# A fused attention, RWKV and feed-forward block on one core: packing small products by quadrant, storing q and k once, and reordering gate and exponential work

## The chip, the cores and the metric

The kernel runs on one core of a Trainium2 chip. The metric is device time in microseconds (us) of one execution. TensorE (PE) does the matrix products, its weight loads (PEld) run beside them; VectorE (DVE) and ScalarE (ACT) read PSUM and do the elementwise work; GpSimd (POOL) and SyncE (SP) issue the DMAs, and POOL does some elementwise work on SBUF.

## The reference

One block of depth 1 on a sequence of 1024 tokens and a width of 1024, in fp32:

```
mod = silu(c) @ w_mod + b_mod                  # six vectors: shift, scale, gate, twice
u   = rms_norm(x) * (1 + scale1) + shift1
proj = u @ w_in                                # q, k, v, f | r, k, v, w, a, g | two gates
o_fox  = causal softmax(q k^T / 8 + cumsum(log f) differences) @ v          # 8 heads of 64
o_rwkv = for each token: state = state * w + (state a) b + v k;  y = state r  # 8 heads of 64
         then a group norm of y, a bonus term and a gate
merged = sigmoid(gate_fox) * (o_fox @ w1) + sigmoid(gate_rwkv) * (o_rwkv @ w2)
h = x + gate1 * (merged @ w_o)
h = h + gate2 * ((silu(conv3(a)) * b) @ w_down)  # a, b = split(modulated rms_norm(h) @ w_up)
out = rms_norm(h) * final_g
```

## The kernel before

Large products are made of two fp32r pieces per operand (`hi`, `lo`) and three 128x128x512 matmuls per tile (`gemm_steps`). The feed-forward block uses seven products per 2x2 block (`OPS`, keys 1 to 7), run by a written list `plan`; `T1` to `T4` are sums of its inputs that are made while the first products run.

The recurrence runs in eight units: four pairs of heads `p` times two halves `hf` of 512 tokens, each half eight chunks of 64 tokens (`NCU` = 8). For each unit there are two generators. `pre` makes decays (`el`, `en` are exponentials of the running sum `cum`), the scaled vectors `ar` and `bk`, the products `p1` of `bk` with `ar` (tile `p` in the trace), and a 31-step elimination on DVE (`t<-E,M` and `E<-E,t`, "the elimination" below), which goes through DRAM before it (`sm`, `M32`) and after it (`se`, `TT`). `main` then does, in this order: a transpose `X` of `TT`, the small products `xi` and `zi`, the products `uw` (copied to `Wt` by DVE and to `UV` by ACT), the products `mz` (read by DVE into `Zt` and `Mt`), the products `sp` and `yp`, and the state chain: for each chunk one product `sp<-S,Mt` on PE and one scaled copy `S` on ACT, each waiting for the one before.

`uw` and `mz` are 16 products each per unit, one for each chunk `c` and head `h`: 64 rows of contraction, 64 output rows, 128 columns, in plain fp32, and the trace shows two matmul records for each. Head 0 lies in partitions 0 to 63 and head 1 in 64 to 127 (`HS`), of the operands and of the PSUM tile alike. Two PSUM tiles are used, the first for chunks 0 to 3, the second for 4 to 7.

The order on PE is fixed by `Weave`: each generator yields how long it would wait, and the time is filled with steps of a queue of large products: first `rkv_items` (r, k, v of the next pair) and `qk_steps` (q and k of attention), then `v_steps`, then the sixteen `gate_steps`, of which the last seven run inside the attention phase (`late_gate`, tile `rk_ps`). On the other engines a scheduler orders the instructions ahead of time, and manual dependencies can pin them; within the attention and the feed-forward phases the written order holds for DVE and ACT.

`qk_steps` leaves a `hi` and a `lo` tile per half (`qh`, `ql`; two buffers with the tag `sp0`) and SP stores them to `d_st` in the layout that attention reads: three copies of 128 rows, each as two DMAs of 64 rows. `load_head` on POOL reads one head back as `stA`, `stB` and `vh`. `gate_steps` evacuates a gate's PSUM bank on ACT and DVE into a tile `gs` with the same tag `sp0`, and stores it to `d_gate`.

Of the kernel before, what the change touches and what calls it, by code (L numbers as in the profile page):

```python
# [9 lines left out]
F32 = mybir.dt.float32  # L10
# [6 lines left out]
S = 1024  # L17
# [115 lines left out]
def hybrid_block(ctx: ExitStack, tc: tile.TileContext, a, out):  # L133
# [13 lines left out]
    def f32(ap):  # L147
        return ap.bitcast(F32)
# [94 lines left out]

    marks = {}
    late_lo = deque()

# [80 lines left out]
    def gate_steps(w, i, pps, ptag, pool, tag):  # L327
        if weave.late == 1:
            yield from late_gate(w, i)
            return  # L330
        for hf in range(2):
            cs = slice(hf * NH, hf * NH + NH)
            ps = pps.tile([128, NH], F32, tag=ptag, name=f"gt{i}_{hf}")
            yield from gemm_steps(ps, w, u, cs)

            g = pool.tile([128, NH], F32, tag=tag, name=f"gs{i}_{hf}")
            nc.scalar.activation(g, ps, AF.Abs)
# [8 lines left out]
    with ExitStack() as es:  # L346
# [39 lines left out]
        def qk_steps(w, i):  # L386
            sc_ = 0.125 if i < 4 else 1.0
            for hf in range(2):
# [6 lines left out]
                stt(lo, ps, sc_, f32(hi), op0=ALU.mult, op1=ALU.subtract)  # L395
                h0 = 2 * (i % 4)
                for t, k, r0 in ((hi, 0, 0), (lo, 0, 64), (hi, 2, 0)) if i < 4 else ((hi, 1, 0), (hi, 1, 64), (lo, 3, 0)):
                    for h in range(2):
                        nc.sync.dma_start(f32(d_st[h0 + h, k, r0 : r0 + 64, cs]), f32(t[h * 64 : h * 64 + 64, :]))

# [157 lines left out]
        with tc.tile_pool(name="lg", bufs=1, reuse_waits="tile") as lg, \  # L558
# [65 lines left out]
            def forget():  # L624
# [10 lines left out]
                for hf in range(2):  # L635
# [27 lines left out]
                    nc.scalar.activation(r[:, 5, :], f32(r[:, 1, :]), AF.Copy, scale=-1.0)  # L663
                    nc.sync.dma_start(f32(d_st[:, 2, 64:68, cs]), f32(r[:, 0:4, :]))
                    nc.sync.dma_start(f32(d_st[:, 3, 64:68, cs]), f32(r[:, 2:6, :]))

# [31 lines left out]
        def pre(k, p, hf):  # L698
# [22 lines left out]
            nc.scalar.activation(en, cum, AF.Exp, scale=DEC)  # L721
            ksq = tmp("ksq")
# [58 lines left out]
            for s in range(31):  # L781
                J, W = s // 4 + 1, 31 - s
                tv = t32[:, 0 : J * W].rearrange("p (j w) -> p j w", w=W)
                tt(tv, E32[:, 0:J, s : s + 1].to_broadcast([128, J, W]),  # L784
                   M32[:, s : s + 1, s + 1 : 32].to_broadcast([128, J, W]), op=ALU.mult)
                tt(E32[:, 0:J, s + 1 : 32], E32[:, 0:J, s + 1 : 32], tv, op=ALU.add)  # L786
# [36 lines left out]
            nc.vector.tensor_copy(QA[:, :, 0, :], c3(q))  # L823
# [3 lines left out]
            tt(bon, bp, vv, op=ALU.mult)  # L827
            units[p, hf] = dict(ready=ready, pcd=pcd, ar=ar, E=E, QA=QA, TT=TT, bon=bon, UV=UV)

        def main(k, p, hf):  # L830
# [31 lines left out]
            Wt = rw.tile([128, NCU, CH], F32, tag="Wt", name=f"Wt{n}", bufs=1)  # L862
            for c0 in range(0, NCU, 4):
                ps = gen(f"uw{n}{c0}")
                for c in range(c0, c0 + 4):
                    for h in range(2):
                        x = (c - c0) * 128
                        mm(ps[HS[h], x : x + 128], TT[HS[h], c, :], QA[HS[h], c, :, :], start=True, stop=True)
                pv = ps.rearrange("p (c a s) -> p c a s", a=2, s=CH)
                nc.vector.tensor_copy(Wt[:, c0 : c0 + 4, :], pv[:, :, 1, :])  # L870
# [4 lines left out]
            for c0 in range(0, NCU, 4):  # L875
                ps = gen(f"mz{n}{c0}")
                for c in range(c0, c0 + 4):
                    for h in range(2):
                        x = (c - c0) * 128
                        mm(ps[HS[h], x : x + 128], Wt[HS[h], c, :], E[HS[h], c, h, 1:3, :], start=True, stop=True)  # L880
                pv = ps.rearrange("p (c a s) -> p c a s", a=2, s=CH)
                tt(Zt[:, c0 : c0 + 4, :], pv[:, :, 0, :], ar[:, 1, c0 : c0 + 4, :], op=ALU.add)
                for h in range(2):
                    tt(Mt[HS[h], c0 : c0 + 4, HS[h]], pv[HS[h], :, 1, :],
                       ident[HS[h], HS[h]].unsqueeze(1).to_broadcast([64, 4, CH]), op=ALU.add)
# [13 lines left out]
            for c in range(last_c + 1):  # L899
                if S[c] is not None:  # L900
                    mm(sp[:, c, :], Mt[:, c, :], S[c], start=False, stop=c == last_c, more=True)
                S.append(rw.tile([128, CH], F32, tag="state", name=f"S{n}{c}", bufs=8))
                marks["S"] = nc.scalar.activation(S[-1], sp[:, c, :], AF.Copy, scale=pcd[:, c : c + 1])
                if c + 1 < NCU:
# [82 lines left out]
    es = ExitStack()  # L987
    at = es.enter_context(tc.tile_pool(name="at", bufs=2, reuse_waits="tile"))
    pl = es.enter_context(tc.tile_pool(name="pl", bufs=2, space=PS))
    pt = es.enter_context(tc.tile_pool(name="pt", bufs=2, space=PS))  # L990
    heads = {}

    def load_head(h):
        A = at.tile([128, 2, S], F32R, tag="stA", name=f"stA{h}")
        nc.gpsimd.dma_start(A, d_st[h, 0:2, :, :].rearrange("k r s -> r k s"))
        B = at.tile([128, 2, S], F32R, tag="stB", name=f"stB{h}")
        nc.gpsimd.dma_start(B[0:68, :, :], d_st[h, 2:4, 0:68, :].rearrange("k r s -> r k s"))
# [1040 lines left out]
```

## Time and profile before

| | us |
|---|---|
| median of three runs | 1654.52 |
| the three runs | 1647.03, 1654.52, 1655.5 |
| the profiled execution | 1648.91 |
| its span | 1647.1 |
| PE busy, share of the span | 1607.8, 98% |
| DVE busy | 1222.6, 74% |
| ACT busy | 820.9, 50% |
| mean clock granted to TensorE | 0.995 |

A row of the timeline is: start in us, length in us, engine, line of the kernel, operation, tile written and tiles read, shape, count; in brackets the idle time of that engine just before it and what ended it. Rows that follow each other with the same text are merged. A group's row has its count, then the busy time and the mean length of one in ns. A row of the waits has the waiting engine and tile, who was waited for, the time in us, how often, and the longest one. From about 160 to 600 us the recurrence runs, from 628 to 820 us attention, and after 1000 us the feed-forward block.

### The profile page before, as it was taken

The page shows a single profiled execution, that of the slowest core. Times are in us where ns is not written, and L with a number is a line of the kernel's source. Part 1 is how long each engine was busy: PE and PEld are TensorE (multiplying, and loading weights), DVE is VectorE, ACT ScalarE, POOL GpSimd, SP SyncE. Part 2 cuts the span into 40 slices and gives each one's busy share as a digit, 9 for nine tenths or more (in the row PEclk, how much of TensorE's full clock was granted, in tenths as well). Part 3 has the DMA queues.
Part 4 walks back from the last instruction along what each step waited for, and adds up shares of the span by engine and source line. Part 5 has one row for each costly group of instructions (what it writes and reads, how often), then busy time and mean ns, then how long its engine had stood idle before and what let it go on. Part 6 is the DMA issues. An engine that isn't in the chain of part 4 may idle for free.

```text
span 1647.1 us, 25947 instructions
## 1 busy us (share of the span) xinstructions
PE 1607.8 (98%) x9694; PEld 1339.6 (81%) x9694; DVE 1222.6 (74%) x2373; ACT 820.9 (50%) x1537; POOL 130.8 (8%) x153
## 2 busy tenths in 40 slices
PE   7999999999999999999999999999999999999998
PEld 7777788798978788888888888788888888888886
DVE  5786787878876526888679447887777777886677
ACT  5563335445445646766623235644444444555455
POOL 0011101111111010221022000000000000000000
PEclk9999999999999999999999999999999999999999
DMA  8488645543332346433197420242232232675363
GB/s 339 138 326 242 178 123 143 134 123 94 107 115 85 97 126 157 129 117 106 56 353 270 168 81 26 84 134 97 96 119 98 96 109 96 225 254 160 122 211 109
DMA packets 121645, 240.59 MB, mean 146 GB/s; under 512 B 40048, under 2 KB 48880, under 8 KB 121520
## 3 DMA queue, kind: packets, MB, share of 16 engines
q1 hardware_dynamic: 113040, 220.58, 41.0%
q0 software_dynamic: 8480, 18.37, 4.2%
q8 instruction: 76, 1.25, 0.3%
q14 instruction: 49, 0.40, 0.1%
HBM read 173.35 MB, written 65.54 MB: 145 GB/s over the span
## 4 chain that ended last, share of the span: by engine, by line
PE 58%; DVE 5%; ACT 2%; DMA 2%; issue 1%; SPq 0%; ACTq 0%; DVEq 0%
PE X L141 13%; PE D L141 13%; PE Y L141 6%; PE wo L141 5%; PE br L141 4%; PE rk_ps L141 3%; PE W L141 3%; PE gt L141 3%; PE lg L141 2%; PE ov L141 2%; PE tp L145 2%; DMA d_gate<-gs 1%; DVE nm L1049 1%; DVE P L1059 1%; DVE tl L1089 0%
## 5 line engine op out<-in xcount | busy, mean ns | idle before, releaser
L141 PE MATMUL D<-op,op 128*128 128x512 f32 x924 | 209.8, 389 | 0.0
L141 PEld LDWEIGHTS D<-op,op 128*128 128x128 f32 x924 | 173.3, 188 | 36.3 <-DVE op L1261 0.3
L141 PE MATMUL X<-T_m,S 128*128 128x512 f32 x440 | 107.8, 390 | 1.6 <-ACT T_m L1722 1.1
L141 PEld LDWEIGHTS X<-T_m,S 128*128 128x128 f32 x440 | 82.4, 188 | 20.4 <-ACT T_m L1722 2.5
L1260 ACT CAST op<-g 128x512 fp32r<-128x512 f32 x77 | 47.8, 621 | 73.8 <-PE D L141 49.0
L1261 DVE TENSOR_TENSOR op<-g,op 128x512 fp32r<-128x512 f32 x77 | 53.0, 688 | 41.4 <-ACT op L1260 41.4
L1519 DVE SCALAR_TENSOR_TENSOR c<-ab,vec,c 128x512 f32<-128x512 f32 x88 | 65.9, 750 | 18.4 <-ACT c L1522 16.8
L784 DVE TENSOR_TENSOR t<-E,M 128x60 f32<-128x60 f32 (+24 forms) x248 | 55.6, 224 | 27.9 <-DMA M<-sm 21.8
L1485 DVE TENSOR_TENSOR A<-ur,A 128x512 fp32r<-128x512 f32 x64 | 44.0, 688 | 38.7 <-ACT A L1481 38.5
L1485 DVE TENSOR_TENSOR S<-ur,S 128x512 fp32r<-128x512 f32 x66 | 45.5, 691 | 35.2 <-ACT S L1481 35.1
L274 DVE TENSOR_TENSOR lo_in<-raw_in,hi_in 128x512 fp32r<-128x512 f32 x84 | 56.7, 712 | 17.6 <-PE gt L141 4.8
L1481 ACT CAST S<-ur 128x512 fp32r<-128x512 f32 x66 | 41.0, 622 | 55.8 <-DVE ur L1474 30.6
L141 PE MATMUL Y<-T_h,S 128*128 128x512 f32 x264 | 63.6, 390 | 0.4 <-ACT T_h L1740 0.4
L141 PE MATMUL Y<-T_h,A 128*128 128x512 f32 x264 | 63.7, 389 | 0.3 <-ACT T_h L1722 0.3
L1053 ACT ACTIVATE P<-lg,nm 128x896 f32<-128x896 f32 (+3 forms) x64 | 47.4, 743 | 30.7 <-DVE nm L1049 22.5
L1481 ACT CAST A<-ur 128x512 fp32r<-128x512 f32 x64 | 39.6, 622 | 43.1 <-PE X L141 31.3
L786 DVE TENSOR_TENSOR E<-E,t 128x60 f32<-128x60 f32 (+24 forms) x248 | 56.2, 227 | 6.4
L141 PE MATMUL W<-B_f,A 128*128 128x512 f32 x252 | 60.6, 389 | 0.0
L141 PE MATMUL X<-B_b,A 128*128 128x512 f32 x252 | 60.5, 389 | 0.0
L141 PEld LDWEIGHTS Y<-T_h,S 128*128 128x128 f32 x264 | 49.5, 188 | 11.1 <-ACT T_h L1740 0.8
L141 PEld LDWEIGHTS Y<-T_h,A 128*128 128x128 f32 x264 | 49.5, 188 | 10.9 <-ACT T_h L1722 0.7
L272 ACT CAST hi_in<-raw_in 128x1024 fp32r<-128x1024 f32 x42 | 43.8, 1048 | 26.3 <-PE ps_rkv L141 11.3
(483 smaller groups left out, 4134.4 us busy)
## 6 DMA issues: line engine op xcount, KB each, us to landing
raw_in<-in_w_in SPq DMA_DIRECT2D x50, 512.0 KB, 4.0
wm<-in_w_mod SPq DMA_DIRECT2D x48, 512.0 KB, 7.3
ur<-in_w_up SPq DMA_DIRECT2D x44, 512.0 KB, 3.8
g<-d_g SPq DMA_DIRECT2D x35, 512.0 KB, 4.0
d_g<-gs SPq DMA_DIRECT2D x44, 256.0 KB, 2.0
d_g<-c SPq DMA_DIRECT2D x33, 256.0 KB, 4.4
d_st<-qh SPq DMA_DIRECT2D x64, 128.0 KB, 2.5
stA<-d_st POOLq DMA_DIRECT2D x8, 1024.0 KB, 6.9
```

The lines of the kernel that those rows point to most:

```text
L141: nc.tensor.matmul(o, lhsT, rhs, start=start, stop=stop, skip_group_check=more)
L145: nc.tensor.transpose(o, i, eye)
L272: nc.scalar.copy(hi, raw)
L274: nc.vector.tensor_tensor(lo[:, c : c + NH], raw[:, c : c + NH], f32(hi[:, c : c + NH]), op=ALU.subtract)
L784: tt(tv, E32[:, 0:J, s : s + 1].to_broadcast([128, J, W]), M32[:, s : s + 1, s + 1 : 32].to_broadcast([128, J, W]), op=ALU.mult)
L786: tt(E32[:, 0:J, s + 1 : 32], E32[:, 0:J, s + 1 : 32], tv, op=ALU.add)
L1053: nc.scalar.activation(e[:, 0:n], lg[:, 0:n], AF.Exp, bias=nm[:, 0:1], accum_out=nm[:, 1:2])
L1260: nc.scalar.copy(hi, src)
L1261: tt(lo, src, f32(hi), op=ALU.subtract)
L1481: nc.scalar.copy(hi, src)
L1485: tt(lo, src, f32(hi), op=ALU.subtract)
L1519: stt(c, ab[:, x + hf * NH : x + hf * NH + NH], V("conv_w", 22 * x + i), c, op0=ALU.mult, op1=ALU.add)
```

## The change

1. `uw` and `mz`: odd chunks write the other half of PSUM's partitions (head 0 to partitions 64 to 127), and the two PSUM tiles now hold the even and the odd chunks. The products alternate between them. The readers follow: for odd chunks each half is read by an instruction of its own, with a shift of 64 partitions. The diff below shows `uw`; `mz` with `Zt` and `Mt` changes in the same way.
2. `d_st` becomes `d_qk`, which holds each `hi` and `lo` tile once, in one DMA of 128 rows, and `d_f` for the forget terms. `load_head` puts the layout together with four DMAs where it had two.
3. `el` and `en` of the next unit, and the last exponential of a gate, are put behind an instruction `S` of a state chain that is under way (`behind_state`, `state_done`): the gate's behind the next `S`, `el` and `en` behind the last.
4. One copy inside `bk` goes from ACT to POOL. In the first unit the first step of the elimination is put behind two DVE instructions (`after_this`).
5. The gates that run after the recurrence but before attention take their `gs` tiles from the attention pool (tag `Ps`), and start behind the gate before.
6. In `plan`, the product (1, 4) is put ahead of (0, 5).

```
     d_gate = dr.tile([16, 128, S], F32, name="d_gate")
-    d_st = dr.tile([8, 4, 128, S], F32R, name="d_st")
+    d_qk = dr.tile([4, 4, 128, S], F32R, name="d_qk")
+    d_f = dr.tile([8, 2, 4, S], F32R, name="d_f")
...
+    def after_this(i):
+        for x in first_step:
+            tc.add_manual_dep(x.ins, i.ins.name, NOSYNC)
+    held = {False: [], True: []}
+    def behind_state(i, next_one=False):
+        if marks.get("chain"):
+            held[next_one].append(i)
+        elif "S" in marks:
+            tc.add_manual_dep(i.ins, marks["S"].ins.name, NOSYNC)
+    def state_done(i, last):
+        marks["S"], marks["chain"] = i, not last
+        for x in held[True] + (held[False] if last else []):
+            tc.add_manual_dep(x.ins, i.ins.name, NOSYNC)
...
-            g = pool.tile([128, NH], F32, tag=tag, name=f"gs{i}_{hf}")
-            nc.scalar.activation(g, ps, AF.Abs)
+            g = marks["spare"].tile([128, NH], F32, tag="Ps", name=f"gs{i}_{hf}", bufs=2) if "spare" in marks else \
+                pool.tile([128, NH], F32, tag=tag, name=f"gs{i}_{hf}")
+            i0 = nc.scalar.activation(g, ps, AF.Abs)
+            if "spare" in marks and "gate_end" in marks:
+                tc.add_manual_dep(i0.ins, marks["gate_end"].ins.name, NOSYNC)
...
-            nc.scalar.activation(g, g, AF.Exp)
+            marks["gate_end"] = nc.scalar.activation(g, g, AF.Exp)
+            behind_state(marks["gate_end"], True)
...
-                for t, k, r0 in ((hi, 0, 0), (lo, 0, 64), (hi, 2, 0)) if i < 4 else ((hi, 1, 0), (hi, 1, 64), (lo, 3, 0)):
-                    for h in range(2):
-                        nc.sync.dma_start(f32(d_st[h0 + h, k, r0 : r0 + 64, cs]), f32(t[h * 64 : h * 64 + 64, :]))
+                for t, x in ((hi, 0), (lo, 1)) if i < 4 else ((hi, 2), (lo, 3)):
+                    nc.sync.dma_start(f32(d_qk[i % 4, x, :, cs]), f32(t))
...
-            nc.scalar.activation(el[:, :, 1:], c3(cum), AF.Exp, scale=-DEC)
+            behind_state(nc.scalar.activation(el[:, :, 1:], c3(cum), AF.Exp, scale=-DEC))
...
-            nc.scalar.copy(bk[64:128, :, 2, :], bk[64:128, :, 0, :])
+            nc.gpsimd.tensor_copy(bk[64:128, :, 2, :], bk[64:128, :, 0, :])
...
-            for c0 in range(0, NCU, 4):
-                ps = gen(f"uw{n}{c0}")
-                for c in range(c0, c0 + 4):
-                    for h in range(2):
-                        x = (c - c0) * 128
-                        mm(ps[HS[h], x : x + 128], TT[HS[h], c, :], QA[HS[h], c, :, :], start=True, stop=True)
-                pv = ps.rearrange("p (c a s) -> p c a s", a=2, s=CH)
-                nc.vector.tensor_copy(Wt[:, c0 : c0 + 4, :], pv[:, :, 1, :])
-                for h in range(2):
-                    nc.scalar.copy(UV[HS[h], c0 : c0 + 4, h, :], pv[HS[h], :, 0, :])
+            ps = [gen(f"uw{n}{e}") for e in range(2)]
+            for c in range(NCU):
+                for h in range(2):
+                    x = c // 2 * 128
+                    mm(ps[c % 2][HS[h ^ c % 2], x : x + 128], TT[HS[h], c, :], QA[HS[h], c, :, :], start=True, stop=True)
+            pv = [x.rearrange("p (c a s) -> p c a s", a=2, s=CH) for x in ps]
+            nc.vector.tensor_copy(Wt[:, 0::2, :], pv[0][:, :, 1, :])
+            for h in range(2):
+                nc.vector.tensor_copy(Wt[HS[h], 1::2, :], pv[1][HS[1 - h], :, 1, :])
+            for e in range(2):
+                for h in range(2):
+                    nc.scalar.copy(UV[HS[h], e::2, h, :], pv[e][HS[h ^ e], :, 0, :])
...
-                marks["S"] = nc.scalar.activation(S[-1], sp[:, c, :], AF.Copy, scale=pcd[:, c : c + 1])
+                state_done(nc.scalar.activation(S[-1], sp[:, c, :], AF.Copy, scale=pcd[:, c : c + 1]), c == last_c)
...
-        nc.gpsimd.dma_start(A, d_st[h, 0:2, :, :].rearrange("k r s -> r k s"))
+        nc.gpsimd.dma_start(A[0:64, :, :], rows[:, 0:3:2, :])
+        nc.gpsimd.dma_start(A[64:128, :, :], rows[:, 1:3, :])
...
-    plan += [(0, 4), (0, 5), (1, 5), (1, 4), (0, 3), (1, 3)] + [(2, k) for k in (1, 7, 6, 2, 4, 5)]
+    plan += [(0, 4), (1, 4), (0, 5), (1, 5), (0, 3), (1, 3)] + [(2, k) for k in (1, 7, 6, 2, 4, 5)]
```

Names in the rows below: a number after a tile's name tells the pair and the half (`uw0_1` is pair 0, half 1), then for `uw` and `mz` which PSUM tile, and last a buffer number. First PE, in the second unit, around `uw`: before, eight products in a row go to each of two PSUM tiles.

```order
L141 MATMUL qk7_0_2827<-u_lo_111,hi_in7_2494 128x512 x6
L141 MATMUL uw0_10_2872<-QA0_1_1844,TT0_1_1986 64x128 x8
L141 MATMUL uw0_14_2884<-QA0_1_1844,TT0_1_1986 64x128 x8
L141 MATMUL qk7_0_2827<-u_hi_110,lo_in7_2495 128x512 x8
L141 MATMUL qk7_1_2914<-u_hi_110,hi_in7_2494 128x512 x6
L141 MATMUL mz0_10_2922<-E0_1_1843,Wt0_1_2871 64x128 x8
L141 MATMUL mz0_14_2934<-E0_1_1843,Wt0_1_2871 64x128 x8
```

After, on the same engine at the same place:

```order
L141 MATMUL qk7_0_2774<-u_lo_112,hi_in7_2449 128x512 x2
L141 MATMUL ssq1_1_2754<-kp1_1_2729,blk_r_1227 128x512 x2
L141 MATMUL qk7_0_2774<-u_lo_112,hi_in7_2449 128x512 x6
L141 MATMUL uw0_10_2819<-QA0_1_1805,TT0_1_1947 64x128 x2
L141 MATMUL uw0_11_2820<-QA0_1_1805,TT0_1_1947 64x128 x2
```

The large products around `uw` stand where they stood; within `uw` two products for one PSUM tile now alternate with two for the other (the last two rows come three times more), and `mz` likewise.

Second SP's queue, in the first unit, where the elimination's input `M320_0` is fetched: before, each `qh` and `ql` tile takes four or two DMAs.

```order
L776 DMA M320_0_1497<-sm0_0_1492 32x1024 x4
L399 DMA d_st_94<-qh5_0_1603 64x512 x4
L399 DMA d_st_94<-ql5_0_1605 64x512 x2
L713 DMA al0_1_1687<-d_lora_101 128x512
L399 DMA d_st_94<-qh5_1_1703 64x512 x4
L399 DMA d_st_94<-ql5_1_1705 64x512 x2
L260 DMA raw_in21_1867<-in_w_in 128x1024
```

After, on the same queue:

```order
L801 DMA M320_0_1474<-sm0_0_1469 32x1024 x4
L424 DMA d_qk_94<-qh5_0_1580 128x512
L424 DMA d_qk_94<-ql5_0_1582 128x512
L738 DMA al0_1_1660<-d_lora_102 128x512
L424 DMA d_qk_94<-qh5_1_1676 128x512
L283 DMA raw_in21_1828<-in_w_in 128x1024
L424 DMA d_qk_94<-ql5_1_1678 128x512
```

Each tile takes one DMA of 128 rows.

Third ACT, in the second unit's state chain (`S0_10` to `S0_16`): before, `el` and `en` of the unit after next and the copy inside `bk` stand ahead of and around its start.

```order
L719 ACTIVATE el2_0_3408<-cum2_0_3402 128x8x64
L740 COPY bk1_1_2864<-bk1_1_2864 64x8x64
L272 CAST hi_in14_3026<-raw_in14_3024 128x1024
L721 ACTIVATE en2_0_3411<-cum2_0_3402 128x512
L903 ACTIVATE S0_10_3010<-sp0_1_2947,pcd0_1_1759 128x64
L393 ACTIVATE qh7_1_3014<-qk7_1_2914 128x512
L692 CAST kr1_1_3340<-ksq1_1_2991 128x512
L903 ACTIVATE S0_11_3038<-sp0_1_2947,pcd0_1_1759 128x64
L903 ACTIVATE S0_12_3047<-sp0_1_2947,pcd0_1_1759 128x64
```

After, on the same engine, the end of that chain:

```order
L935 ACTIVATE S0_15_3029<-sp0_1_2892,pcd0_1_1728 128x64
L748 ACTIVATE ksq2_0_3354<-k20_2714,vec_72 128x512
L935 ACTIVATE S0_16_3049<-sp0_1_2892,pcd0_1_1728 128x64
L744 ACTIVATE el2_0_3349<-cum2_0_3343 128x8x64
L746 ACTIVATE en2_0_3352<-cum2_0_3343 128x512
L947 COPY y0_1_3073<-yp0_1_2891 128x512
L717 CAST Ztr0_1_3088<-y0_1_3073 128x512
```

`el2_0` and `en2_0` now stand behind the last `S` and ahead of the copy `y`, and the copy of `bk` is gone from ACT.

More of the change, by code (lines that the diff above doesn't have):

```diff
@@ L244, in hybrid_block @@
     marks = {}
+    first_step = []
+    def after_this(i):
[11 more added lines that the diff above has]
+            tc.add_manual_dep(x.ins, i.ins.name, NOSYNC)
+        held[True].clear()
+        if last:
+            held[False].clear()
     late_lo = deque()
@@ L663, in forget @@
                     nc.scalar.activation(r[:, 5, :], f32(r[:, 1, :]), AF.Copy, scale=-1.0)
-                    nc.sync.dma_start(f32(d_st[:, 2, 64:68, cs]), f32(r[:, 0:4, :]))
-                    nc.sync.dma_start(f32(d_st[:, 3, 64:68, cs]), f32(r[:, 2:6, :]))
+                    nc.sync.dma_start(f32(d_f[:, 0, :, cs]), f32(r[:, 0:4, :]))
+                    nc.sync.dma_start(f32(d_f[:, 1, :, cs]), f32(r[:, 2:6, :]))
             for p in range(4):
@@ L783, in pre @@
                 tv = t32[:, 0 : J * W].rearrange("p (j w) -> p j w", w=W)
-                tt(tv, E32[:, 0:J, s : s + 1].to_broadcast([128, J, W]),
-                   M32[:, s : s + 1, s + 1 : 32].to_broadcast([128, J, W]), op=ALU.mult)
+                i = tt(tv, E32[:, 0:J, s : s + 1].to_broadcast([128, J, W]),
+                       M32[:, s : s + 1, s + 1 : 32].to_broadcast([128, J, W]), op=ALU.mult)
+                if k == 0 and s == 0:
+                    first_step.append(i)
                 tt(E32[:, 0:J, s + 1 : 32], E32[:, 0:J, s + 1 : 32], tv, op=ALU.add)
@@ L826, in pre @@
             bon = tmp("bon", bufs=2)
-            tt(bon, bp, vv, op=ALU.mult)
+            after_this(tt(bon, bp, vv, op=ALU.mult))
+            first_step.clear()
             units[p, hf] = dict(ready=ready, pcd=pcd, ar=ar, E=E, QA=QA, TT=TT, bon=bon, UV=UV)
@@ L873, in main @@
             yield 2970
             Zt = rw.tile([128, NCU, CH], F32, tag="Zt", name=f"Zt{n}", bufs=1)
-            for c0 in range(0, NCU, 4):
-                ps = gen(f"mz{n}{c0}")
-                for c in range(c0, c0 + 4):
-                    for h in range(2):
[L879 to L882, printed above, removed]
-                for h in range(2):
-                    tt(Mt[HS[h], c0 : c0 + 4, HS[h]], pv[HS[h], :, 1, :],
+            ps = [gen(f"mz{n}{e}") for e in range(2)]
@@ new lines, in main @@
+            for c in range(NCU):
+                for h in range(2):
+                    x = c // 2 * 128
+                    mm(ps[c % 2][HS[h ^ c % 2], x : x + 128], Wt[HS[h], c, :], E[HS[h], c, h, 1:3, :], start=True, stop=True)
+            pv = [x.rearrange("p (c a s) -> p c a s", a=2, s=CH) for x in ps]
+            tt(Zt[:, 0::2, :], pv[0][:, :, 0, :], ar[:, 1, 0::2, :], op=ALU.add)
+            for h in range(2):
+                tt(Zt[HS[h], 1::2, :], pv[1][HS[1 - h], :, 0, :], ar[HS[h], 1, 1::2, :], op=ALU.add)
@@ L885, in main @@
+            for e in range(2):
+                for h in range(2):
+                    tt(Mt[HS[h], e::2, HS[h]], pv[e][HS[h ^ e], :, 1, :],
                        ident[HS[h], HS[h]].unsqueeze(1).to_broadcast([64, 4, CH]), op=ALU.add)
@@ L993, in load_head @@
     def load_head(h):
+        rows = d_qk[h // 2, :, h % 2 * 64 : h % 2 * 64 + 64, :].rearrange("k r s -> r k s")
         A = at.tile([128, 2, S], F32R, tag="stA", name=f"stA{h}")
-        nc.gpsimd.dma_start(A, d_st[h, 0:2, :, :].rearrange("k r s -> r k s"))
+        nc.gpsimd.dma_start(A[0:64, :, :], rows[:, 0:3:2, :])
+        nc.gpsimd.dma_start(A[64:128, :, :], rows[:, 1:3, :])
         B = at.tile([128, 2, S], F32R, tag="stB", name=f"stB{h}")
-        nc.gpsimd.dma_start(B[0:68, :, :], d_st[h, 2:4, 0:68, :].rearrange("k r s -> r k s"))
+        nc.gpsimd.dma_start(B[0:64, :, :], rows[:, 0:4:3, :])
+        nc.gpsimd.dma_start(B[64:68, :, :], d_f[h].rearrange("k r s -> r k s"))
         vh = at.tile([128, 8, 128], F32R, tag="vh", name=f"vh{h}")
```

6 lines of the change are left out of this document (3 added, 3 removed).

## The prediction

> **What bounds the kernel now.** I read the head of the profile page first, then the waits of PE, then the timeline at the places the diff touches.
>
> ```profile
> span 1647.1 us, 25947 instructions
> PE 1607.8 (98%) x9694; PEld 1339.6 (81%) x9694; DVE 1222.6 (74%) x2373; ACT 820.9 (50%) x1537; POOL 130.8 (8%) x153
> ```
>
> TensorE is busy for 1607.8 of 1647.1 us, so 39.3 us are idle. Time can be won in three ways: less PE work, less PE idle, or a better clock while PE works. The waits of PE tell which part of the idle the change can reach:
>
> ```profile
> PE idle L141 <- DMA cst<-in_cst: 6.4, 1, 6.4
> PE rk_ps L141 <- ACT gm L1163: 3.1, 3, 1.9
> PE sp L141 <- ACT S L903: 2.8, 4, 1.4
> PE qk L141 <- DVE ql L395: 2.3, 1, 2.3
> PE ov L141 <- DVE o L1122: 2.0, 1, 2.0
> PE X L141 <- ACT T_m L1722: 1.1, 2, 0.9
> ```
>
> The start (6.4) is untouched. The rows of `rk_ps`, `sp`, `qk` and `X` are each reached by one edit; they hold 9.3 us. After a wait the clock can matter too:
>
> ```profile
> 190.00:200.00 10.00, 10.00 (x39) 8.13 (x38) 9.69 (x28) 4.05 (x6) 0.97 (x3) 0.86 0.73 189
> 620.00:630.00 10.00, 8.07 (x29) 6.27 (x29) 3.02 (x5) 3.38 (x6) 1.04 (x1) 0.83 1.21 243
> 670.00:680.00 10.00, 8.02 (x54) 6.96 (x52) 9.63 (x20) 8.53 (x18) 0.08 (x1) 1.00 0.72 193
> ```
>
> In these rows the window is followed by its length, then busy time of PE, PEld, DVE, ACT and POOL, then the granted clock. Behind the `qk` wait it is 0.86, around the `rk_ps` wait 0.83. The window from 670 us has as much idle time (2.0 us) and keeps 1.00, so idleness alone does not decide it.
>
> **Part 1, packing `uw` and `mz` (T1).** The cost of a product in the array is the spacing of records, not their modelled length.
>
> ```profile
> 281.18 1.96 PE L141 MATMUL uw<-QA,TT 64*64 64x128 f32 x32
> 283.08 2.14 PE L141 MATMUL qk<-u_hi,lo_in 128*128 128x512 f32 x8
> 281.18 0.33 PE L141 MATMUL uw<-QA,TT 64*64 64x128 f32 x2
> 170.70 0.27 PE L145 MATMUL vt<-cst,v 128*128 128x128 f32 x1
> 170.81 0.27 PE L145 MATMUL at<-cst,ar 128*128 128x128 f32 x1
> 288.58 0.29 PE L141 MATMUL yp<-E,UV 128*64 128x64 f32 x4
> 288.69 0.29 PE L141 MATMUL sp<-UV,E 128*64 128x64 f32 x4
> 226.99 0.69 PE L141 MATMUL xi<-X,E 32*32 32x32 f32 x32
> ```
>
> Full-array records of 128 columns in plain fp32 stand 0.11 us apart (170.70, 170.81). The 32 records of one `uw` stage take 281.18 to 283.08, which is 1.90; at 0.11 each they would take 3.52, so two run at a time, one per head, on the two diagonal quadrants of the array. The third row, from a window of 0.1 us, shows the two starting together. The two other quadrants idle. After the change, the products of an odd chunk keep their rows but take the other columns, so four quadrants can work. Two rows bear on whether they will. Column halves with different moving data already work side by side: four records of `yp`, at half the columns, take 288.58 to 288.69, two slots of 0.055 and not four. And the issue of records is not the limit: 32 of `xi` fit into 0.69, 0.022 each, while four quadrants need one per 0.11/4 = 0.028. So 16 slots per stage become 8, and 8 × 0.11 = 0.88 per stage are saved; two stages in eight units make 16, and T1 = 14.1. All of it is PE time in a stretch where PE is the bound (windows there have 10.00 of 10.00). The bounds are 14.1 and, below nothing, the cost of changing diagonals: the 32 records are 16 × 0.11 = 1.76 of the 1.90 up to the next shape, so a change of shape costs at most 0.14. If each of the 7 changes per stage cost that and nothing overlapped, 7 × 0.14 × 16 = 15.7 would be lost. I take 14.1, since the nearest rows, `xi` and `yp`, pay no such change between neighbours.
>
> The Trainium skill ("TensorE: Matmul & The Clock Gate", Part 3, The mechanism) says that matmuls start and end strictly in program order, without reordering. By that rule the second pass of an fp32 product would hold back the product behind it, T1 would be 0 and the sum 14.1 smaller; the trace, where records of two products seem to start within 0.01 us, speaks against it but does not label the passes, so it is a rival below.
>
> **Part 2, `d_qk` and the first unit (T2).**
>
> ```profile
> 178.68 3.30 SPq L399 DMA_DIRECT2D d_st<-qh  x4
> 182.54 0.19 DVE L784 TENSOR_TENSOR t<-E,M 128x31 f32<-128x31 f32 x1 [6.66 <-DMA M<-sm]
> 183.94 0.60 ACT L393 ACTIVATE qh<-qk 128x512 fp32r<-128x512 f32 x1 [4.17 <-DVE E L786]
> 187.14 0.69 DVE L274 TENSOR_TENSOR lo_in<-raw_in,hi_in 128x512 fp32r<-128x512 f32 x1
> 188.49 0.68 DVE L395 SCALAR_TENSOR_TENSOR ql<-qk,qh 128x512 fp32r<-128x512 f32 x1
> 189.22 3.61 PE L141 MATMUL qk<-u_hi,hi_in 128*128 128x512 f32 x8 [2.31 <-DVE ql L395]
> 182.65 1.98 PE L141 MATMUL qk<-u_lo,hi_in 128*128 128x512 f32 x8
> ```
>
> PE needs the bank that `ql` frees; `ql` came at 188.49 because `qh` and `ql` share two buffers, whose stores took four and two DMAs (3.30 us of SP's queue for `qh` alone), and because it stands deep in the elimination on DVE. Now each store is one DMA, about 3.30/4 = 0.8, and `ql` stands behind the first step (182.54) and two `lo_in` pieces (0.69 each), which with `qh` at 183.94 or sooner gives some 185: 3 us earlier, more than the wait. So 2.31 go. The eight matmuls behind it took 3.61 where eight take 1.98, another 1.63 by the clock. T2 = 2.31 + 1.63 = 3.9, bounds 2.3 and 3.9. Next late there is nothing for PE: `bon` and the `QA` copy, now ahead of the elimination's first step, fill DVE's wait for `M`. The four DMAs of `load_head` instead of two go on POOL's queue, busy 8% of the span; I cost them at nothing, and if they delayed the first head, the price would be like the `ov` wait above, 2.0.
>
> **Part 3, the gates' tiles (T3).**
>
> ```profile
> 609.63 0.68 ACT L932 ACTIVATE rs<-va,epsr 128x512 f32<-128x512 f32 x1
> 610.72 0.63 ACT L933 ACTIVATE rs<-rs 128x512 f32<-128x512 f32 x1
> 618.05 0.60 ACT L337 ACTIVATE gs<-gt 128x512 f32<-128x512 f32 x1 [4.64 <-DMA d_gate<-gs]
> 621.27 0.58 ACT L1162 ACTIVATE gs<-rk_ps 128x512 f32<-128x512 f32 x1
> 622.39 3.33 PE L141 MATMUL rk_ps<-u_hi,hi_in 128*128 128x512 f32 x8 [1.93 <-ACT gm L1163]
> 625.51 2.40 PE L141 MATMUL rk_ps<-u_lo,hi_in 128*128 128x512 f32 x8
> ```
>
> The last gate waited 4.64 for the store of an earlier `gs`, so the `rk_ps` evacuation came late and PE waited 1.93. Two slow groups followed: (3.33 − 1.98) + (2.40 − 1.98) = 1.8. With `gs` in tiles of the attention pool that wait goes, and the chain behind it (618.05 to 621.27) starts earlier. But the gate ahead of it now stands behind two `rs` (0.68 and 0.63), its tile lies in memory that the recurrence gives up only then, and the later gate must wait for its end: I let as much, 1.3, of the 1.93 stay. T3 lies between 0.6 (1.93 − 1.3, clock as before) and 3.7 (1.93 + 1.8, all). I take 1.8, about half, because a shorter idle time may still cost some clock.
>
> The Trainium skill (same page, HAM oscillation) has the clock fall only for idle gaps over about 3.4 us. By it gaps of 2.31 and 1.93 would have cost no clock: T2 = 2.3, T3 = 0.6, and the sum 2.8 smaller. The trace disagrees at these two gaps (0.86 and 0.83), and agrees at 670 us (1.00).
>
> **Part 4, exponentials behind the chain (T4).**
>
> ```profile
> 296.47 0.63 ACT L721 ACTIVATE en<-cum 128x512 f32<-128x512 f32 x1 [0.21 <-DVE bk L744]
> 297.01 0.29 ACT L903 ACTIVATE S<-sp,pcd 128x64 f32<-128x64 f32 x1
> 297.36 0.43 PE L141 MATMUL sp<-S,Mt 128*128 128x64 f32 x2 [1.38 <-ACT S L903]
> 298.19 0.32 ACT L903 ACTIVATE S<-sp,pcd 128x64 f32<-128x64 f32 x1
> ```
>
> `en` stood ahead of `S`, and PE waited 1.38. Behind the chain's end it cannot. Of the four such waits (2.8) I take this one and a third of the rest: T4 = 1.9, between 0.5 (another ACT job steps in) and 2.8. A link of the chain takes 1.2 us (297.01 to 298.19), so over its seven or eight links the exponentials come up to 10 us later; they are read in the next unit, and eight units share about 440 us. The `y` copy behind them waits some 0.6 per exponential, and `bk` on POOL (8% busy) may take longer; both have that much time, so no price. If the cover fails, it is one `en` per unit, 8 × 0.63 = 5.0, which I count with the new waits below.
>
> **Part 5, `plan` (T5).**
>
> ```profile
> 1033.36 1.02 PE L141 MATMUL X<-T_m,S 128*128 128x512 f32 x2 [0.90 <-ACT T_m L1722]
> ```
>
> (1, 4) ahead of (0, 5) gives `T_m` one product more of time (12 matmuls, near 3 us at 1.98 for eight), but the sums come from a DVE that is full there. T5 = 0.6, from 0 to 1.5.
>
> **Part 6, new waits (T6).**
>
> ```profile
> 284.00 0.42 DVE L870 COPY Wt<-uw 128x256 f32<-128x256 f32 x1
> 285.00 0.42 DVE L870 COPY Wt<-uw 128x256 f32<-128x256 f32 x1
> 286.52 1.96 PE L141 MATMUL mz<-E,Wt 64*64 64x128 f32 x32
> ```
>
> `Wt` took two copies, one during and one after `uw`; now all three wait for the end of `uw`, which comes 0.88 earlier. `Zt` also gets a third instruction: 2 × 0.42 more DVE per unit. The last `Wt` copy ended at 285.42, 1.1 us ahead of `mz` at 286.52; the third takes 0.4 of that and the shorter filler the rest here and there. Over eight units I put 1.0 on it, 0.5 on the last pair (its `q` and `tb` products stand between `uw` and `mz` and need banks that are freed later), and 0.5 on the first unit's elimination. T6 = −2.0, from 0 to −5.0.
>
> **The sum.** 14.1 + 3.9 + 1.8 + 1.9 + 0.6 − 2.0 = 20.3, against the profiled execution's 1648.9: 1628.6. That execution lies near the fast end of the three runs (1647.03 to 1655.5), 5.6 below their median. I can't tell which end the runs of after fall to, so I add half, 2.8: **1631**.
>
> **The rivals.**
>
> R1, passes strictly in order. Each fp32 product has two records on its own quadrant; if the second must wait for the first and nothing may pass it, only two quadrants work at any time, as now. T1 = 0, the sum 6.2: 1642.7, with the 2.8 as above 1645.5. For it: no row of before has four quadrants at once with 128 columns. Against it: two `uw` records start together, and a strict order would begin with one alone.
>
> R2, slower: changing diagonals drains the array. Now every second product changes it, 7 times a stage; at 0.14 each T1 = −15.7, so 1628.6 + 14.1 + 15.7 = 1658.4, and 1661 with the 2.8. It decides from about 0.13 per change, where it outweighs the 6.2 of the rest by 8.3. For it: 0.14 is what the end of a stage leaves over. Against it: `yp` and `sp` alternate with 0.11 per four records, no more than two slots.
>
> R3, new waits: the stages are shorter but `mz` stands waiting for `Wt`, and half of T1 comes back as idle time: 1628.6 + 7 + 2.8 = 1638. For it: DVE has 9.69 of 10 in the window at 190 us. Against it: the 1.1 us of slack.
>
> **How the numbers follow.** Forecast 0.68, R3 0.10, R1 0.12, R2 0.10. A measurement of this kernel can tell about 0.5%, 8.3 us. The forecast and R3 are faster by more (0.78), R1, a gain of 6.2, lies within it (0.12), R2 is slower (0.10). With every gain at its upper end and no new wait the sum is 26.0, so 1622.9; an execution at the fast end is 1.9 lower: 1621. The upper end takes in R3 and R1: 1645. Left out are R2 and the tails.
>
> **What would show it.** Right: a `uw` stage of 1.0 us instead of 1.90, and no `qk` wait near 187 us; 190 to 200 us at a clock near 1.00; no `sp` wait over 1 us; PE busy near 1590. R1 leaves the stage at 1.9, R2 makes it over 2.5, R3 shows PE idle ahead of `mz`. The forecast is wrong if a stage is above 1.4, or if the elimination's chain on DVE, 31 steps per unit, sets the end of the units, so that shorter PE work only turns into idle time before `xi`.

## The result and the profile after

The changed kernel is slower: 1657.11 us median of nine runs (1655.79 to 1659.67) against 1648.72 for before in nine runs; the ratio is 1.0047, 95% interval 1.0033 to 1.0061. The forecast was 1631. The profiled execution took 1656.44.

The head of the page:

```profile
span 1654.7 us, 25934 instructions
PE 1600.8 (97%) x9694; PEld 1330.3 (80%) x9694; DVE 1229.2 (74%) x2389; ACT 816.2 (49%) x1529; POOL 144.9 (9%) x177
```

The waits of PE (waiting tile, who was waited for, us in total, times, longest):

```profile
PE q L141 <- DVE QA L838: 6.0, 2, 3.1
PE sp L141 <- ACT S L935: 3.8, 4, 2.0
PE v L141 <- DVE vs L987: 3.6, 3, 2.3
...
PE mu L141 <- DVE E L789: 2.3, 1, 2.3
PE rk_ps L141 <- ACT gm L1199: 2.3, 3, 1.2
```

PE has 7 us less to do, but 53.9 us idle (1654.7 − 1600.8) where it had 39.3 (1647.1 − 1607.8). The forecast had PE busy near 1590. The packing itself did what it says. From the timeline:

```profile
280.63 1.10 PE L141 MATMUL uw<-QA,TT 64*64 64x128 f32 x32
281.66 2.14 PE L141 MATMUL qk<-u_hi,lo_in 128*128 128x512 f32 x8
...
228.75 0.34 PE L141 MATMUL uw<-QA,TT 64*64 64x128 f32 x4
```

And the groups by form:

```profile
L141 PE MATMUL uw<-QA,TT 64*64 64x128 f32 x256 | 8.8, 275 | 0.0
L141 PE MATMUL mz<-E,Wt 64*64 64x128 f32 x256 | 11.0, 277 | 0.4 <-ACT E L845 0.2 <-ACT UV L902 0.2
```

A stage of 32 records takes 1.03 us (280.63 to 281.66) instead of 1.90; in a window of 0.06 us (third row) four records start, where two did. The busy time of `uw` and `mz` together fell from 31.4 to 19.8. The stall near 187 us is gone too: the window from 190 us has the clock at 1.00, where it was 0.86. Windows of the changed kernel (length, busy time of PE, PEld, DVE, ACT and POOL, granted clock):

```profile
190.00:200.00 10.00, 10.00 (x61) 7.89 (x61) 9.81 (x24) 4.13 (x6) 2.08 (x3) 1.00 0.42 132
230.00:280.00 50.00, 44.45 (x424) 35.59 (x424) 40.51 (x116) 22.01 (x43) 7.84 (x10) 1.00 0.36 107
280.00:330.00 50.00, 45.39 (x432) 36.34 (x430) 38.50 (x108) 21.15 (x41) 8.55 (x13) 0.97 0.38 111
330.00:380.00 50.00, 45.53 (x532) 40.77 (x531) 41.42 (x117) 21.21 (x45) 6.15 (x9) 0.97 0.43 117
```

The time is lost from 230 to 380 us: PE is busy 135.4 of 150 us there, and twice the mean clock is 0.97. Before:

```profile
230.00:380.00 150.00, 147.75 (x1547) 124.78 (x1545) 123.00 (x348) 71.98 (x141) 21.35 (x30) 1.00 0.47 127
```

The changed kernel is ahead when the stretch begins (the first `xi` starts at 221.68 us, before at 226.99) and behind when it ends (the fourth at 379.10, before at 371.39). The new waits cost more than their own length. Behind three of the five PE waits over 1.9 us that the recurrence now has, those that end at 315.22, 370.53 and 449.11, the granted clock is one half for 3.41 us, as it was in before behind the `qk` wait. The changed kernel's three stretches, then the one of before:

```profile
316.72:320.13 3.41, 3.41 (x40) 2.55 (x40) 3.31 (x7) 0.92 (x2) 0.00 (x0) 0.50 0.44 102
371.33:374.74 3.41, 3.41 (x19) 2.71 (x15) 3.15 (x10) 1.06 (x2) 1.28 (x1) 0.50 0.57 181
449.84:453.25 3.41, 3.41 (x19) 3.41 (x18) 3.31 (x8) 0.83 (x2) 1.28 (x1) 0.50 0.48 144
```

```profile
189.45:192.86 3.41, 3.41 (x9) 2.66 (x9) 3.03 (x13) 0.40 (x1) 0.00 (x0) 0.50 0.65 144
```

Half the clock for 3.41 us is 1.7 us of PE work, by an estimate. Behind the other two waits (2.89 and 1.98 us) the clock stayed; what decides it is not shown.

The wait that is new is at the head of DVE's queue. Two places of the changed kernel's timeline, with rows of SP's queue (`SPq`), ACT, DVE and PE picked out in order of time:

```profile
256.17 0.62 ACT L746 ACTIVATE en<-cum 128x512 f32<-128x512 f32 x1
259.45 0.43 SPq L736 DMA_DIRECT2D cum<-d_lora  x1
263.84 1.27 DVE L740 TENSOR_TENSOR_SCAN cum<-cst,cum 128x256 f32<-128x256 f32 x2 [3.15 <-DMA cum<-d_lora]
265.03 1.70 DVE L838 COPY QA<-at 64x256 f32<-64x256 f32 x4
266.88 0.33 PE L141 MATMUL q<-UV,E 64*64 64x64 f32 x4 [2.89 <-DVE QA L838]
...
309.68 0.45 SPq L736 DMA_DIRECT2D cum<-d_lora  x1
313.21 1.28 DVE L740 TENSOR_TENSOR_SCAN cum<-cst,cum 128x256 f32<-128x256 f32 x2 [6.98 <-DMA cum<-d_lora]
315.22 0.47 PE L141 MATMUL mu<-Ztr,blk_r 128*128 128x512 f32 x1 [2.34 <-DVE E L789]
```

The same step before:

```profile
249.74 0.64 ACT L721 ACTIVATE en<-cum 128x512 f32<-128x512 f32 x1 [0.79 <-DVE bk L744]
250.40 0.33 SPq L711 DMA_DIRECT2D cum<-d_lora  x1
253.52 1.26 DVE L715 TENSOR_TENSOR_SCAN cum<-cst,cum 128x256 f32<-128x256 f32 x2
```

There is one buffer `cum`, and `en` is its last reader. Before, the load of the next `cum` went out at 250.40, 0.02 us after `en` ended. Now `en` ends at 256.79, the load goes out at 259.45, behind other transfers on SP's queue, and the running sum, whose place in DVE's order was set ahead of time, stands there until 263.84. `QA` and the next `E` are queued behind it, and PE waits for these.

### The profile page after: what moved, and what is told of

It reads as the page before. It is cut to its first block, busy times and chain, and to the rows that moved or that the text cites. A ratio compares the mean times of both kernels' runs of the same rounds, so it can differ in the third digit from the quotient of the medians.

```text
span 1654.7 us, 25934 instructions
## 1 busy us (share of the span) xinstructions
PE 1600.8 (97%) x9694; PEld 1330.3 (80%) x9694; DVE 1229.2 (74%) x2389; ACT 816.2 (49%) x1529; POOL 144.9 (9%) x177
## 4 chain that ended last, share of the span: by engine, by line
PE 66%; DVE 9%; DMA 3%; ACT 2%; issue 1%; SPq 1%; POOL 0%; DVEq 0%; ACTq 0%; POOLq 0%
PE X L141 13%; PE D L141 13%; PE Y L141 7%; PE wo L141 5%; PE br L141 5%; PE gt L141 5%; PE W L141 3%; PE ps_rkv L141 3%; PE rk_ps L141 3%; PE lg L141 2%; PE ov L141 2%; PE tp L145 2%; DVE t L809 1%; DVE E L813 1%; DMA M<-sm 1%
## 5 line engine op out<-in xcount | busy, mean ns | idle before, releaser
L809 DVE TENSOR_TENSOR t<-E,M 128x60 f32<-128x60 f32 (+24 forms) x248 | 56.6, 228 | 20.8 <-DMA M<-sm 14.6
```

The costliest lines, as they stand in the source:

```text
L809: i = tt(tv, E32[:, 0:J, s : s + 1].to_broadcast([128, J, W]), M32[:, s : s + 1, s + 1 : 32].to_broadcast([128, J, W]), op=ALU.mult)
```

## The experiments

In the theories' letters, H is this held buffer, and W has the saved PE time come back as waits for DVE. Each time is a median; a ratio is to the runs of before on the same chips (medians 1648.5 to 1649.5).

**The moved exponentials.** Undone in the changed kernel:

```
-            behind_state(nc.scalar.activation(en, cum, AF.Exp, scale=DEC))
+            nc.scalar.activation(en, cum, AF.Exp, scale=DEC)
```

and `el` likewise.

> The changed kernel with el and en no longer put behind the state chain (the gate's exponential still is). H, held buffer: en is the last reader of cum, so moving it 12 us later holds the one cum buffer, its next load goes out late, and the scan in DVE's queue waits for it with the E and QA instructions behind it; then DVE's waits for cum fall from 20.4 us towards the 11.2 of before, PE's waits for QA (6.0) and for E at mu (2.3) go, and the time is 1636 to 1646. W, the packed stages outrun DVE: the elimination on DVE sets the end of the units, the waits only change their names, 1654 to 1658.

1649.63, ratio 1.0007 (0.9995 to 1.0018): 7.5 us come back by the medians, though not the 11 or more that H expected. DVE's waits for the load of `cum`, in before, in the changed kernel and in this one:

```profile
DVE cum L715 <- DMA cum<-d_lora: 11.2, 4, 4.7
```

```profile
DVE cum L740 <- DMA cum<-d_lora: 20.4, 6, 7.0
```

```profile
DVE cum L740 <- DMA cum<-d_lora: 6.4, 4, 3.4
```

Whether it is the buffer or the place of the exponentials, the next kernel tells; it leaves them behind the chain:

```
+            en = tmp("en")
...
-                nc.vector.tensor_tensor_scan(cum[:, c0 : c0 + 256], cst2[:, 128:384], cum[:, c0 : c0 + 256], initial=0.0,
+                nc.vector.tensor_tensor_scan(en[:, c0 : c0 + 256], cst2[:, 128:384], cum[:, c0 : c0 + 256], initial=0.0,
...
-            behind_state(nc.scalar.activation(en, cum, AF.Exp, scale=DEC))
...
+            behind_state(nc.scalar.activation(en, en, AF.Exp, scale=DEC))
```

> The changed kernel with the exponentials left behind the chain, but the running sum written into the tile of en (el reads it there, en is made in place), so that cum is free as soon as the sum is made and its next load can go out at once. H: DVE's wait for the load of cum is nearly gone in spite of the late exponentials, and the time is that of the kernel with el and en put back, within 4: 1636 to 1648. W: 1654 to 1658. If not the held buffer but the exponentials' place among other ACT work costs the time, this stays at 1654 to 1658 while the kernel with el and en put back gains.

1650.97, ratio 1.0014 (1.0003 to 1.0025): 6.1 of the 7.5 us come back although `el` and `en` still run late, and DVE has no wait for the load of `cum` left. That is within 4 of the kernel with `el` and `en` put back, though above the range that H gave. And alone on before:

> The kernel before with el and en behind the state chain and nothing else. H, held buffer: the load of cum goes out some 10 us later in units 3 to 6, DVE's waits for it rise from 11 to about 20 us, and the time is 7 us more than before: 1654 to 1658. If the loss needs the other edits beside it: 1647 to 1651.

1656.56, ratio 1.0048 (1.0031 to 1.0065), with DVE's waits at twice those of before:

```profile
DVE cum L731 <- DMA cum<-d_lora: 22.0, 7, 8.3
```

H is shown: this edit alone costs what the whole change costs, and freeing `cum` takes the cost away.

**The packing.** Alone on before:

> The kernel before with the packing of uw and mz alone. H: nothing of the packing itself is at fault; the stages take 1.0 us instead of 1.9 and 9 to 14 of the 14.1 arrive: 1634 to 1640 where before is 1648.7. W: the gain is taken back by waits for DVE: 1645 to 1650, with PE idle 10 us longer than the 39 of before.

1647.94, ratio 0.9997 (0.9988 to 1.0006). Taken out of the changed kernel:

> The changed kernel with uw and mz as before the change. H: the loss by the held buffer stays and the gain of the packing goes: 1663 to 1672. W: little or no loss against the changed kernel, 1655 to 1660, since the packed stages brought only waits.

1657.17, as the changed kernel. So 12 us less of PE work are worth about nothing in either setting, as W had it by the time. PE idle in the profiled execution is 46.2 us (1643.5 − 1597.3), 7 more than before, where W said 10; that execution is the fastest of its twelve (1645.35). Where `xi` starts in three units that follow each other, before and then with the packing alone:

```profile
274.48 0.69 PE L141 MATMUL xi<-X,E 32*32 32x32 f32 x32
323.18 0.69 PE L141 MATMUL xi<-X,E 32*32 32x32 f32 x32
371.39 0.69 PE L141 MATMUL xi<-X,E 32*32 32x32 f32 x32
```

```profile
274.50 0.69 PE L141 MATMUL xi<-X,E 32*32 32x32 f32 x32
323.06 0.69 PE L141 MATMUL xi<-X,E 32*32 32x32 f32 x32
371.42 0.69 PE L141 MATMUL xi<-X,E 32*32 32x32 f32 x32
```

96.9 us for two units in both, though a packed unit has 1.5 us less PE work. In this stretch the saved time stands as waits; the largest, in the packed kernel:

```profile
294.46 0.63 ACT L719 ACTIVATE el<-cum 128x512 f32<-128x512 f32 x1 [6.91 <-DVE ar L741]
295.00 1.03 ACT L272 CAST hi_in<-raw_in 128x1024 fp32r<-128x1024 f32 x1
296.05 0.61 ACT L740 COPY bk<-bk 64x512 f32<-64x512 f32 x1
296.69 0.31 ACT L907 ACTIVATE S<-sp,pcd 128x64 f32<-128x64 f32 x1
297.06 0.43 PE L141 MATMUL sp<-S,Mt 128*128 128x64 f32 x2 [2.35 <-ACT S L907]
```

Its window from 288 us, with all engines as above:

```profile
288.00:300.00 12.00, 9.65 (x81) 7.67 (x77) 11.66 (x33) 4.64 (x9) 0.74 (x2) 1.00 0.39 91
```

PE waits for `S`, `S` stands behind `el`, a cast and the copy of `bk` on ACT, and `el` waits for `ar` on DVE, which is busy 11.66 of 12 us. In before the same window, and the one in the unit ahead, are just as full:

```profile
240.00:252.00 12.00, 11.70 (x123) 9.69 (x119) 11.81 (x30) 5.34 (x10) 0.57 (x2) 1.00 0.23 82
288.00:300.00 12.00, 10.62 (x112) 8.71 (x109) 11.75 (x31) 4.66 (x9) 1.42 (x2) 1.00 0.42 107
```

Three causes were tried. First the work on DVE (D), against the state chain (C): the instructions that the packing adds there, without the packing:

```
-                nc.vector.tensor_copy(Wt[:, c0 : c0 + 4, :], pv[:, :, 1, :])
+                for y in (slice(0, 128),) if c0 == 0 else HS:
+                    nc.vector.tensor_copy(Wt[y, c0 : c0 + 4, :], pv[y, :, 1, :])
```

and `Zt` likewise.

> The kernel before, unpacked, with the instructions that the packing adds on DVE: the second Wt copy and the second Zt addition of a unit are made in two halves of 64 partitions, 16 instructions of 0.42 us more, nothing else changed. D: they cost most of their 6.7 us, 1652 to 1656, and the packing itself is then worth 5 to 9 us on PE. C: DVE has room, 1648 to 1650.

1653.55, ratio 1.0034 (1.0021 to 1.0047): 5 us more, in D's range. But the traces also show DVE's other instructions in another order than before, so the added work and the new order are not told apart. Then the packing with the odd `Wt` copies on ACT (`nc.scalar.copy` for `nc.vector.tensor_copy`):

> The kernel before with the packing, but the two copies of the odd chunks into Wt run on ACT, so that DVE has as much to do as before the packing in this step (one Wt copy instead of two, three Zt additions instead of two). D, DVE is the bound between mz and the next p (it is busy 12 of 12 us from 240 to 252 us, before and with the packing), so PE time saved there is waited away and each DVE instruction more costs its own time: DVE busy falls from 1230 to about 1224 us and the time from 1648 to 1641 to 1645. C, the state chain between PE and ACT is the bound instead (PE's waits for S went from 2.8 to 6.1 us): ACT has more to do, 1647 to 1651.

1647.33, ratio 0.9991 (0.9982 to 1.0000). DVE is back at 1223.8 us and still nothing comes out, against D and within C. Nor when the two steps on `al` are left out on both sides, or made on POOL (`nc.gpsimd`):

```
-            ts(al, al, V("k_a", p), oka[:, p : p + 1], op0=ALU.mult, op1=ALU.add)
-            tt(al, al, kk, op=ALU.mult)
```

> The kernel before, unpacked, with two DVE instructions of each unit left out, those that scale al and multiply it by k (0.54 and 0.69 us, in the stretch where DVE is busy 11.8 of 12 us); bk's second part is then made of the wrong vector. It is the yardstick for the next kernel. D: DVE and PE are both at their limit there, so some of the 9.8 us of DVE work comes out: 1643 to 1647. C: 1647 to 1649.

> The packing, with the same two DVE instructions of each unit left out. D, DVE paces the recurrence and swallows the PE time that the packing saves: with DVE relieved the packing is worth 6 us or more against the kernel that has the same two left out and no packing, 1636 to 1641. C, the state chain between PE and ACT is the limit whatever DVE does: at most 2 us between the two, 1645 to 1649.

> The packing, with these two instructions made on POOL, which is busy 8% of the span, with the whole result computed. D: as with the two left out, less what POOL's slower instructions add to the way to bk: 1638 to 1645. C: 1646 to 1650. If POOL takes several us for the two, p comes late and it is slower: 1650 or more.

1655.47, 1659.11 and 1658.78 (ratios 1.0042, 1.0064 and 1.0068, all clear of 1). Fewer instructions on DVE made both kernels slower, which no theory of mine had. As a plain sum of DVE work D doesn't hold. But leaving an instruction out also shifts the order that the scheduler sets on DVE, so whether DVE's work would count in a fixed order is not shown. Which shift costs the 7 us was not followed up; in the first of the three, 2.3 us are lost ahead of the first `xi` (229.29 us, before 226.99).

Second the queue ahead of `S` (S), against waits that turn up anywhere (O): with `el` and `en` late, the sum in `en`'s tile, and the cast `kr` of the bonus term behind the chain too.

```
-            nc.scalar.copy(hi, x)
+            i = nc.scalar.copy(hi, x)
+            if late:
+                behind_state(i)
```

> The changed kernel with the running sum in en's tile (el and en behind the chain without holding cum), and with the cast kr of the bonus term put behind the state chain as well. S, what stands ahead of S in ACT's queue is where the packing's gain goes: PE's waits for S fall from 5.2 us to under 2.5 and the time from 1651 to 1643 to 1648. O, the saved time turns up as another wait wherever the next engine is late: 1649 to 1652, waits for S fewer and others more.

> The same with uw and mz unpacked. S: 5 to 10 us slower than its packed twin, 1650 to 1656. O: within 2 us of it.

> The kernel before with the running sum in en's tile and el, en and the cast kr behind the state chain, nothing else. H: without the held buffer the moved exponentials cost nothing, where they cost 8 us alone: 1646 to 1650. S: the 2.8 us of waits for S mostly go, 1645 to 1648.

> The same with the packing. S: the packing is worth 5 us or more beside its unpacked twin, 1637 to 1643, faster than both kernels. O: within 2 us of the twin, 1645 to 1650.

1650.67 packed and 1647.52 unpacked on the changed kernel; 1646.98 and 1646.46 on before. So in the first pair the packing costs 3 us, more than O's 2, and in the second it is worth nothing. PE's waits of the first of these:

```profile
PE mu L141 <- POOL Wtr L720: 4.5, 3, 2.6
...
PE v L141 <- DVE vs L989: 3.1, 2, 2.3
...
PE sp L141 <- ACT S L937: 1.1, 1, 1.1
```

The wait for `S` is 1.1 us, where the kernel with the sum in `en`'s tile alone had 5.2, and waits for `mu` rose from 1.3 to 4.5: O. The third kernel (ratio 0.9986, 0.9974 to 0.9997) agrees with H: with `cum` free, and `kr` late too, the late exponentials cost nothing. It and its packed twin (0.9985, 0.9974 to 0.9996) are the only kernels with the whole result whose interval lies below 1, by 0.15%.

Third the elimination's loop (L), with 16 steps instead of 31:

```
-            for s in range(31):
+            for s in range(16):
```

> The kernel before with the elimination cut from 31 to 16 steps (30 of 62 DVE instructions of a unit left out, the result of those rows not computed). L, the loop of the elimination and PE are both just in time: PE's own work then sets the units and little is gained, 1640 to 1648, with PE's idle in the recurrence nearly gone. If the loop alone set the pace, 10 us or more would come out: under 1638.

> The packing with the same 16 steps. L: with the loop shorter the packing comes through, 7 to 13 us below its unpacked twin. O, whatever DVE does the saved time turns into waits by the order of the queues: within 3 us of the twin.

1646.32, ratio 0.9985 (0.9975 to 0.9995), and 1642.20, ratio 0.9956 (0.9940 to 0.9971). Halving the chain is worth 3 us alone, though PE's idle time from 160 to 600 us is 6.8 us (440.00 − 433.17 busy) where before has 7.1, not nearly gone as L had it. Beside the short chain the packing is worth 4, the only setting in which a packed kernel is clearly faster than its twin. That is between L's 7 and O's 3: as far as these two kernels tell, the loop takes part of the saved time, not all of it.

One part can be read from the clock of the runs. In all six pairs of a kernel without and with the packing, the packed runs have the lower mean granted clock, by 0.0015 to 0.0026 (0.9956 and 0.9939 for the packing alone). A stretch of 3.41 us at half the clock is 0.001 of the mean, so this is one to three such stretches more, and at most 2.5 to 4.3 us of the 12 by an estimate (the difference times 1650 us). That these follow from the new waits is likely but not shown. The rest stays open.

**The other edits**, each alone on before: `d_qk` with `after_this`, and the gates' tiles.

> The kernel before with q and k stored once and the first unit's elimination behind its two DVE instructions. As the prediction had it, the wait of 2.3 us and the slow matmuls behind it go and 3.9 stay won: 1644 to 1646. D: PE gets ahead by some 4 us and waits for DVE in the next units (sp behind S, q behind QA, v behind vs), so that 0 to 1.5 are left: 1647 to 1650.

1648.56, ratio 1.0006 (0.9996 to 1.0016). Its waits of PE no longer have the row of `qk`, but:

```profile
PE sp L141 <- ACT S L911: 4.4, 4, 2.4
PE rk_ps L141 <- ACT gm L1174: 4.1, 3, 3.0
```

where before had 2.8 and 3.1. Of 2.3 us taken away 2.6 stand elsewhere. The gain does arrive at its place, and is used up in the next units: the second `xi` starts at 271.07 us where before has 274.48, the third at 322.41 where before has 323.18.

> The kernel before with the last gates' tiles in the attention pool and each gate behind the one before, nothing else. As the prediction had it: 1.8 us won, the wait for gm falls from 1.9 to 1.3 and the two slow groups behind it are mostly gone: 1646 to 1648. If the wait there depends on when the store of the gate lands and moves by a microsecond or two from one kernel to the next (1.2, 1.9, 2.8 and 3.0 in the kernels so far), nothing that can be told: 1648 to 1650.

1648.95, ratio 1.0004 (0.9996 to 1.0013). The longest `rk_ps` wait is 1.2 there, but it is 1.2 in the kernel with the packing alone too, and 2.8 in the one with DVE's instructions split: it moves with the whole program.

The four edits that were run alone sum up: −0.03% (packing), +0.48% (exponentials), +0.06% and +0.04% are +0.55%, the whole change +0.47%. The copy of `bk` on POOL, the gate's exponential and the plan were not run alone.

## Why the prediction was wrong

**Part 4 put the loss at nothing.** The forecast was a gain of 1.9. The prediction moved `el` and `en` later, asked only when they are read ("in the next unit"), and gave their lateness no term in the sum; if the cover failed it put 5.0 on what they hold up on ACT. It did not ask what they read. They hold `cum`, and the price was 8 us alone (1656.56 against 1648.5). Before's own rows showed it: the load of `cum` leaves SP at 250.40, right behind the end of `en`. This alone is as large as the whole loss. The wait that part 4 meant to take away did not go either: 3.8 us for `S` instead of 2.8. The longest, 1.98 us until 299.84, has the cast `kr` ahead of `S`:

```profile
298.95 0.62 ACT L717 CAST kr<-ksq 128x512 fp32r<-128x512 f32 x1 [3.79 <-DVE ksq L773]
299.48 0.31 ACT L935 ACTIVATE S<-sp,pcd 128x64 f32<-128x64 f32 x1
```

**Part 1 was right about the array and wrong about the time, and is the largest miss.** Of its 14.1 us about 1 arrived when the packing ran alone (1647.94 against 1649.12). A stage takes 1.03 us; 0.88 was forecast as the saving, 0.87 came. R1 and R2 are out: four records start together, and changing the diagonal costs nothing that shows. The Trainium skill's rule of strict order ("TensorE: Matmul & The Clock Gate", Part 3, The mechanism) would, as the prediction read it for the two records of a product, have had the stage stay at 1.9; with four quadrants at once that reading is refuted here. The rule itself, the order of starts and ends, was not tested. The sentence that failed is that this was "PE time in a stretch where PE is the bound", read from PE busy 10.00 of 10.00; the row with that figure, from 190 us, has DVE at 9.69 as well. In the stretch behind `mz` PE is busy 11.70 and DVE 11.81 of 12 us. I read it as two engines at their limit, where relief of one is worth little; the runs show that the time did not come, not that DVE's load alone is why.

**Part 6 was mis-sized.** New waits were put at −2.0, down to −5.0. PE's idle time rose by 7 us with the packing alone and by 14.6 with the whole change. The part also counted waits by their length alone: the prediction gave 1.63 us of clock to the `qk` wait that goes, and nothing to waits that come, though three of the new ones have the clock at one half behind them. R3 came nearest, with a chance of 0.10, but not by its mechanism: it had `mz` wait for `Wt`, and PE's idle time ahead of `mz` is 0.4 us in the changed kernel. The time came back as waits for `QA`, `vs`, `E` and `S`.

**Parts 2 and 3 were right at the place and wrong at the end.** The `qk` wait and its slow matmuls are gone, `rk_ps` waits 1.2 and 0.5 instead of 1.9; the kernels with these edits alone gain nothing. Part 5's swap took away the wait for `T_m` and put another sum in its place:

```profile
PE X L141 <- DVE Ze_a L1602: 1.4, 2, 1.2
```

**The forecast's own test** named a chain on DVE that "sets the end of the units, so that shorter PE work only turns into idle time". The idle time came about, though not ahead of `xi` (0.2 us); the kernels with 16 steps show that the chain is at most part of it.

## What to carry to other kernels

An instruction that is moved later also holds its inputs longer: look for the transfer that waits for that buffer, and for what is queued behind the transfer's reader. A wait that is taken away can save the slow clock behind it, and a new wait can bring one: price both. A PE that is busy all the time in a stretch is the bound only if no other engine there is; put the windows of all engines beside each other before PE time is counted as time. Where each engine runs a fixed order, test an edit alone before its saving is added up.

## What was not expected of the hardware

All four 64x64 quadrants work at once on different products: 32 records of 128 columns in plain fp32 take 1.03 us where two quadrants took 1.90, with the next products alternating between the diagonals. Waits of PE that lasted 2.31 to 3.07 us were followed by 3.41 us at half the clock, and one of 2.89 was not. And 16 fewer instructions on DVE, which also changed the order of the others, made the program slower: 1655.47 against 1648.5.
